# The recurrence's products in another shape, merge parts between its stages, and modulation pieces moved later, in a one-layer attention, recurrence and feed-forward block

## The chip, the cores and the metric

One Trainium2 chip, one NeuronCore. The metric is the device time of one execution of the program, in microseconds (us). TensorE (PE in the profile) multiplies; VectorE (DVE) and ScalarE (ACT) do the elementwise work; SyncE (SP) only issues the transfers; GpSimd (POOL) has nothing to do.

## The reference, cut to what matters

All numbers are float32, for 256 tokens of width 2048. The conditioning vector `c` gives six modulation rows of 2048 numbers, and the token mixer has two branches, an attention (three kinds of it, added with gates) and a gated linear recurrence, whose outputs are merged:

```python
c_act = jax.nn.silu(c)
mod = c_act @ ada_w[l] + ada_b[l]                  # 2048 x 12288
sh1, sc1, g1, sh2, sc2, g2 = jnp.split(mod, 6)
h = rmsnorm(x, norm1_g[l]) * (1.0 + sc1) + sh1
# token mixer
z = h @ w_in                                       # 2048 x 13360
q, kc, vc, ks, vs, kw, vw, g_nsa, lx, ly, ga, gb = jnp.split(z, ...)
o_a = nsa_attention(q, kc, vc, ks, vs, kw, vw, g_nsa, ...)
u = causal_dwconv(lx, conv_w, conv_b)
o_b = jax.nn.gelu(ly) * rg_lru(u, w_a, b_a, w_i, b_i, lam)
merged = jax.nn.sigmoid(ga) * (o_a @ proj_a) + jax.nn.sigmoid(gb) * (o_b @ proj_b)
y = merged @ w_out
# and behind it
x = x + g1 * y
h = rmsnorm(x, norm2_g[l]) * (1.0 + sc2) + sh2
x = x + g2 * conv_glu_ffn(h, ffn_up[l], ffn_conv_w[l], ffn_conv_b[l], ffn_down[l])
return rmsnorm(x, final_g)
```

`rg_lru` makes two gates from `u` by 128-wide blocks, and from them the coefficients of a scan over the tokens.

## The kernel before, in words

**Numbers.** A float32 product is made of three products in a shorter format that the array takes in one pass: each operand is a high part `hi` (ACT's copy into the short format) and a low part `lo` (DVE's difference), and hi·hi, hi·lo and lo·hi are added in PSUM. An activation such as `h1` holds its two parts side by side, columns 0 to 255 and 256 to 511.

**Weights.** Every weight comes once, in pieces of 128 x 2048 numbers (1 MB): `stage` takes one of four `raw` slots and `load` issues the transfer on SyncE's queue, in program order. `split` makes `hi` and `lo` of half a piece (L107 ACT, L108 DVE), in three buffers each, at a raised priority. `bank` gives one of four PSUM banks of 512 columns.

**Products.** `dense_pair` (feed-forward, L114) makes for each 128 x 128 block of weights one product of `hi` with all 512 columns and one of `lo` with 256; the two 256-column halves of a bank are added later (`reduce`). Its order is fixed by `keep_in_program_order`. `dense_pair1` (L172, used 16 times, by the recurrence alone) makes three products of 256 columns for each block, two of `hi` and one of `lo`, into one bank for both of its outputs f. `dense_tok` (L192) has the tokens as the stationary operand and 512 columns of weights moving, 96 products for a call with four pieces.

**Modulation.** `ada_piece` (L232) stages one piece of `ada_w` in a `raw` slot, and DVE multiplies it with the row of `silu(c)` and sums (L234), then adds the offset (L235). `filler(n)` takes the next n of 64 pieces of the list `fill`, in the order g1, sc2, sh2, g2. The rows have due times: g1 and sc2 before the output projection ends its first part, sh2 before the feed-forward part, g2 behind it.

**Order.** A planner orders each engine's instructions ahead of time by priority, which is program order, and by when operands and slots are free; a queue is worked off in that order. Behind the first projections come four query products with an attention unit each, then eight rounds `pr` of a recurrence input `lx` (`dense_pair1`), a further attention unit in the first four, and `filler(2)`. `attention(g, t)` makes scores for four heads, one after the other, softmax (L676 to L686), transposes, and the product with the values into `oA`. Then four recurrence stages `bt` run: convolutions on DVE (L740, L743), gate products (L745, L747), Sigmoid, Tanh, Exp and Sqrt on ACT in an order fixed by `tbl` (each kind needs its table loaded), the scan (L762), and two rounds of `ly` with Gelu into `oB`. The merge loops over four column blocks n and the branches s: gates (for n = 0 they were made earlier and lie in `mq`), Sigmoid (L792), the product with `oA` or `oB`, `filler`, and behind both the sum and its transposes. The output projection (four `dense_tok`) adds to x, squares, and writes the transposed result into `hp`.

**Slots.** SBUF tiles of one tag share one place. C0 to C7 hold in turn the compressed keys' operands (`gat`, `gath`), `cmpb`, the probabilities' transposes `pT`, the recurrence's `lx` (C4 to C7) and `oB`.

## Time and profile before

| | |
|---|---|
| median of 3 runs | 1792.68 us (1792.08 to 1794.26) |
| the profiled execution | 1793.77 us |
| its span | 1792.0 us |
| instructions | 25746 |
| mean TensorE clock granted | 0.997 of 2.4 GHz |
| read from HBM | 425.72 MB, 239 GB/s over the span |

The span is the time from the first to the last instruction of the program in the profiled execution; the rest of its time lies around it. In the profile a line such as L107 or L53 can be that of a helper (`split`, `load`), and the names are those of the tiles. Products overlap in the array and their ends are modelled, so the distance from start to start tells more than a duration. PEld is the load of the stationary operand, which runs beside the products.

### The profile page before, as it was taken

To read this page: it belongs to the slowest core of one execution; us is meant where nothing else is said; L and a number is where in the kernel's file an instruction comes from. 1 tells how busy PE (TensorE), PEld (TensorE's weight loads), DVE (VectorE), ACT (ScalarE), POOL (GpSimd) and SP (SyncE) were. 2 spreads that over 40 slices of the span, in tenths; PEclk is the share of its full clock that TensorE was granted. 3 is DMA by queue.
4 is the path that set the end of the run, shared out by engine and by line. 5 is a ranking of instruction groups with operands and counts; after the bars stand their busy time and mean duration, and the time that the engine had idled before them with its cause. 6 is when DMAs were issued, how large, how long until landed. Compare 5 with 4: busy or idle time off the path is not lost.

```text
span 1792.0 us, 25746 instructions
## 1 busy us (share of the span) xinstructions
PE 1771.6 (99%) x10262; PEld 1545.9 (86%) x10262; DVE 1350.5 (75%) x1976; ACT 881.9 (49%) x1202; POOL 0.2 (0%) x4
## 2 busy tenths in 40 slices
PE   8999999999999999999999999999999999999997
PEld 7999898888999888888888998888888888888886
DVE  7998897998698766767765997888555677766555
ACT  5644464655578444444445644444433444444443
POOL 0000000000000000000000000000000000000000
PEclk9999999999999999999999999999999999999999
DMA  9999864665646867777775566777655555555552
GB/s 350 379 335 355 288 245 161 235 212 203 221 173 227 303 237 290 286 292 281 294 266 195 186 235 235 282 282 282 239 193 200 191 188 188 188 188 188 190 198 106
DMA packets 64200, 429.50 MB, mean 240 GB/s; under 512 B 7088, under 2 KB 7376, under 8 KB 15568
## 3 DMA queue, kind: packets, MB, share of 16 engines
q1 hardware_dynamic: 63792, 427.08, 66.2%
q8 instruction: 80, 1.31, 0.3%
q10 hardware_dynamic: 288, 0.79, 0.1%
q14 instruction: 40, 0.33, 0.1%
HBM read 425.72 MB, written 2.11 MB: 239 GB/s over the span
## 4 chain that ended last, share of the span: by engine, by line
PE 86%; DVE 6%; DMA 4%; issue 2%; ACT 2%; SPq 0%; DVEq 0%; ACTq 0%
PE P L130 26%; PE P L204 12%; PE P L205 12%; PE P L203 12%; PE P L187 3%; PE P L188 3%; PE P L185 3%; DMA raw<-ada_w 2%; DVE lo L108 2%; PE P L464 2%; PE P L466 2%; PE P L465 2%; PE P L149 1%; PE P L148 1%; PE P L150 1%
## 5 line engine op out<-in xcount | busy, mean ns | idle before, releaser
L107 ACT ACTIVATE hi<-raw 128x1024 fp32r<-128x1024 f32 x588 | 622.0, 1060 | 764.5 <-PE P L205 325.5
L108 DVE TENSOR_TENSOR lo<-raw,hi 128x1024 fp32r<-128x1024 f32 x588 | 717.1, 1222 | 370.5 <-ACT hi L107 369.7
L130 PE MATMUL P<-h,hi 128*128 128x512 f32 x1344 | 463.9, 394 | 0.0
L130 PE MATMUL P<-h,lo 128*128 128x256 f32 x1344 | 366.4, 278 | 0.0
L130 PEld LDWEIGHTS P<-h,hi 128*128 128x128 f32 x1344 | 249.1, 188 | 54.9
L130 PEld LDWEIGHTS P<-h,lo 128*128 128x128 f32 x1344 | 252.4, 188 | 4.2
L234 DVE SCALAR_TENSOR_TENSOR raw<-raw,crow 128x2048 f32<-128x2048 f32 x64 | 146.2, 2285 | 3.6 <-DMA raw<-ada_w 3.2
L188 PE MATMUL P<-h,lo 128*128 128x256 f32 x512 | 147.6, 289 | 0.8 <-DVE lo L108 0.8
L187 PE MATMUL P<-h,hi 128*128 128x256 f32 x512 | 146.7, 287 | 0.0
L185 PE MATMUL P<-h,hi 128*128 128x256 f32 x512 | 146.7, 287 | 0.0
L464 PE MATMUL P<-h,hi 128*128 128x256 f32 x384 | 107.9, 285 | 0.3 <-ACT hi L107 0.3
L465 PE MATMUL P<-h,hi 128*128 128x256 f32 x384 | 107.6, 284 | 0.0
L466 PE MATMUL P<-h,lo 128*128 128x256 f32 x384 | 102.2, 284 | 0.0
L188 PEld LDWEIGHTS P<-h,lo 128*128 128x128 f32 x512 | 97.8, 191 | 1.8 <-DVE lo L108 1.4
L187 PEld LDWEIGHTS P<-h,hi 128*128 128x128 f32 x512 | 97.9, 191 | 1.4 <-issue 1.2
L185 PEld LDWEIGHTS P<-h,hi 128*128 128x128 f32 x512 | 97.9, 191 | 1.0 <-issue 0.7
L204 PE MATMUL P<-lo,ua 128*128 128x512 f32 x240 | 93.5, 390 | 0.3 <-DVE lo L108 0.3
L205 PE MATMUL P<-hi,ua 128*128 128x512 f32 x240 | 93.4, 389 | 0.0
L203 PE MATMUL P<-hi,ua 128*128 128x512 f32 x240 | 83.6, 389 | 0.0
L204 PE MATMUL P<-lo,h 128*128 128x512 f32 x192 | 75.5, 393 | 0.0
L464 PEld LDWEIGHTS P<-h,hi 128*128 128x128 f32 x384 | 74.0, 193 | 1.1 <-ACT hi L107 0.5
L205 PE MATMUL P<-hi,h 128*128 128x512 f32 x192 | 74.9, 390 | 0.0
(281 smaller groups left out, 3131.6 us busy)
## 6 DMA issues: line engine op xcount, KB each, us to landing
raw<-ada_w SPq DMA_DIRECT2D x96, 1024.0 KB, 5.0
raw<-w_up SPq DMA_DIRECT2D x96, 1024.0 KB, 4.8
raw<-w_down SPq DMA_DIRECT2D x48, 1024.0 KB, 4.9
raw<-w_lru SPq DMA_DIRECT2D x32, 1024.0 KB, 4.9
raw<-w_proj SPq DMA_DIRECT2D x32, 1024.0 KB, 5.1
raw<-w_gates SPq DMA_DIRECT2D x24, 1024.0 KB, 6.5
raw<-w_out SPq DMA_DIRECT2D x16, 1024.0 KB, 4.9
raw<-w_kv SPq DMA_DIRECT2D x24, 512.0 KB, 6.7
```

Of the source, the lines that this page charges most:

```text
L107: A.activation(hi[:, :n], raw[:, lo_col:lo_col + n], AF.Copy)
L108: V.tensor_tensor(lo[:, :n], raw[:, lo_col:lo_col + n], hi[:, :n].bitcast(F32), op=ALU.subtract)
L130: PE.matmul(ps[f][:, 0:256] if w else ps[f], hl[w][:, k * 256 + f * 128:k * 256 + f * 128 + 128], r[:, 0:256] if w else r, start=(kt == 0 ...
L185: PE.matmul(o, hi[:, sl], r[:, 0:256], start=(kt == 0 and f == 0), stop=False, skip_group_check=True)
L187: PE.matmul(o, hi[:, sl], r[:, 256:512], start=False, stop=False, skip_group_check=True)
L188: PE.matmul(o, lo[:, sl], r[:, 0:256], start=False, stop=(kt == n - 1), skip_group_check=True)
L203: PE.matmul(ps[j], xh, hi[:, w], start=(kt == 0), stop=False, skip_group_check=True)
L204: PE.matmul(ps[j], xh, lo[:, w], start=False, stop=False, skip_group_check=True)
L205: PE.matmul(ps[j], xl, hi[:, w], start=False, stop=(kt == n - 1), skip_group_check=True)
L234: V.scalar_tensor_tensor(raw, raw, 1.0, row, op0=ALU.mult, op1=ALU.mult, accum_out=modc[:, c:c + 1])
L464: PE.matmul(o, hi[:, sl], h1[:, kt, 0:256], start=first and f % 2 == 0, stop=False, skip_group_check=True)
L465: PE.matmul(o, hi[:, sl], h1[:, kt, 256:512], start=False, stop=False, skip_group_check=True)
```

## The change

It touches six things. `dense_pair1` goes; the recurrence's 16 products are made by `dense_pair` with `pinned=False`, which leaves their order to the planner, and `add_halves` takes each bank out with a copy on ACT and an addition on DVE. The first merge parts move up between the recurrence stages: behind the scan of stages 0 and 2 the product of branch 0 with `oA` for n = 0 and 1, behind that of stages 1 and 3 the gates for n = 1; their Sigmoids, and those of `mq`, are put into the `tbl` order behind the next stage's Tanh. The modulation pieces are called for inside `dense_tok`, behind the weight pieces that `fills` lists, and fewer of them early: 24 are left behind the merge instead of 16. In attention, the heads' probabilities are scaled and transposed in pairs, with max, reciprocal and gate once for each pair. `cmpb` goes to C3, `gat` to C7, `gath` to C2, C4, C5 and C6; `w2t`, `hs`, the first head's `p` and `gp` share one buffer `xp` of twice the size instead of two. The last columns of `hp` are written behind the output projection instead of ahead of it.

```diff
-        def dense_pair(pieces, rhs):
+        def dense_pair(pieces, rhs, pinned=True):
...
-                    for w in (0, 0, 1, 0, 1, 0, 1, 1) + (0, 1) * 4 if ip + half == 0 else (0, 1) * 8:
+                    for w in (0, 0, 1, 0, 1, 0, 1, 1) + (0, 1) * 4 if pinned and ip + half == 0 else (0, 1) * 8:
...
+                        if pinned:
+                            tc.keep_in_program_order(mm)
             return ps
+
+        def add_halves(dst, p):
+            A.activation(dst, p[:, 256:512], AF.Copy)
+            with tc.high_priority(200):
+                V.tensor_tensor(dst, p[:, 0:256], dst, op=ALU.add)
...
-        def dense_pair1(pieces, rhs):
...
-        def dense_tok(pieces, lhs, late=None):
+        def dense_tok(pieces, lhs, late=None, fills=()):
...
                     for j in range(2):
                         products(j, k0, *hl)
+                if ip in fills:
+                    filler()
...
-        cmpb = big.tile([128, 1024], F32R, tag="C7", name="cmpb")
+        cmpb = big.tile([128, 1024], F32R, tag="C3", name="cmpb")
...
-        w2t = tmp.tile([128, 2, 128], F32, tag="xp", bufs=2, name="w2t")
+        wh = tmp.tile([128, 2, 256], F32, tag="xp", bufs=1, name="wh")
+        w2t = wh[:, 0].rearrange("p (j e) -> p j e", j=2)
...
-                g = big.tile([128, 16, 4, NCMP], F32, tag="C6", name="gat")
+                g = big.tile([128, 16, 4, NCMP], F32, tag="C7", name="gat")
...
+            def turn_heads(hh):
+                p = heads[hh]
+                for b in range(2):
+                    pb = p[:, b * nk:b * nk + nk]
+                    V.tensor_scalar(pb, pb, sm[:, 1, hh, b:b + 1], None, op0=ALU.mult)
+                tp = psx.tile([128, 512], F32, tag="t", bufs=1, name="tp")
+                for j in range(nj):
+                    PE.transpose(tp[:, j * 128:j * 128 + 128], p[:, j * 128:j * 128 + 128], ident)
+                for n in range(t + 1):
+                    A.activation(pT[n][:, :, hh, :], tp[:, n * 256:n * 256 + 256].rearrange("p (j q) -> p j q", q=128),
+                                 AF.Copy)
...
+                p = tmp.tile([128, 512], F32, tag=("xp", "r", "iu", "tt")[hh], bufs=1, name="p")
...
+                if hh % 2 == 0:
+                    continue
+                w = sm[:, 1, hh - 1:hh + 1]
+                V.tensor_scalar(w, w, 1e-30, None, op0=ALU.max)
+                V.reciprocal(w, w)
+                V.tensor_tensor(w, w, gates[:, hh - 1:hh + 1, 1:3], op=ALU.mult)
+                turn_heads(hh - 1)
+                turn_heads(hh)
...
         for pr in range(8):
-            pl = dense_pair1([w_lru[pr, k] for k in range(2)], h1r)
...
+            ps = dense_pair([w_lru[pr, k] for k in range(2)], h1r, False)
+            for f in range(2):
+                add_halves(lx[pr // 2][:, 2 * (pr % 2) + f], ps[f])
             if units:
                 attention(*units.pop(0))
-            filler(2)
+            filler()
...
+        def gates_of(n, s, fills):
+            if n == 0:
+                gated[n, s] = [mq[s][:, j] for j in range(2)]
+                return gated[n, s]
+            gated[n, s] = [tmp.tile([128, 512], F32, tag=(("r", "iu"), ("u", "tt"))[s][j], bufs=1, name="sg")
+                           for j in range(2)]
+            return dense_tok([w_gates[n - 1, s, k] for k in range(4)], h1r, fills=fills)
+
+        def open_gates(n, s, ps):
+            for j in range(2):
+                tbl(A.activation(gated[n, s][j], ps[j], AF.Sigmoid))
+
+        def multiply(n, s, fills):
+            rhs = (lambda kt: oB[kt // 2][:, kt % 2]) if s else (lambda kt: oA[:, kt])
+            ps = dense_tok([w_proj[n, s, k] for k in range(4)], rhs, fills=fills)
+            for j in range(2):
+                V.tensor_tensor(gated[n, s][j], ps[j], gated[n, s][j], op=ALU.mult)
+
+        waiting = [(0, s, gates_of(0, s, ())) for s in range(2)]
...
+            while waiting:
+                open_gates(*waiting.pop(0))
             tbl(A.activation(r, r, AF.Exp, scale=-2.0))
...
+            if bt % 2 == 0:
+                multiply(bt // 2, 0, (1,))
+            else:
+                waiting.append((1, bt // 2, gates_of(1, bt // 2, (1,))))
             for h in range(2):
...
-                pl = dense_pair1([w_lru[8 + pr, k] for k in range(2)], h1r)
+                ps = dense_pair([w_lru[8 + pr, k] for k in range(2)], h1r, False)
                 gl = u[:, 2 * h:2 * h + 2]
-                tbl(A.activation(gl, pl.rearrange("p (f t) -> p f t", f=2), AF.Gelu_apprx_tanh))
+                for f in range(2):
+                    add_halves(gl[:, f], ps[f])
+                tbl(A.activation(gl, gl, AF.Gelu_apprx_tanh))
...
-                filler(2 if pr % 4 == 0 else 0)
...
+            for s in range(2):
+                if (n, s) not in gated:
+                    open_gates(n, s, gates_of(n, s, (1, 3) if s else (0, 1, 3)))
+                if s == 1 or n > 1:
+                    multiply(n, s, (0, 1, 3))
...
-        filler(max(0, len(fill) - 16))
+        assert len(fill) == 24
...
-            ps = dense_tok([w_out[n, k] for k in range(4)], lambda kt: mg[kt // 2][:, kt % 2])
+            ps = dense_tok([w_out[n, k] for k in range(4)], lambda kt: mg[kt // 2][:, kt % 2],
+                           fills=(0, 1, 3) if n < 2 else (0, 2) if n == 2 else ())
...
-                    gp = tmp.tile([128, 256], F32, tag="xp", bufs=2, name="gp")
+                    gps = tmp.tile([128, 2, 256], F32, tag="xp", bufs=1, name="gp") if f == 0 else gps
+                    gp = gps[:, f]
```

## Rows read from the trace of the kernel before

**Rows 1.** The page of the profile: busy time, share of the span and instructions of each engine; and from the 40 slices the TensorE clock granted, in tenths of full speed (2.4 GHz).
```profile
PE 1771.6 (99%) x10262; PEld 1545.9 (86%) x10262; DVE 1350.5 (75%) x1976; ACT 881.9 (49%) x1202; POOL 0.2 (0%) x4
...
PEclk9999999999999999999999999999999999999999
```

**Rows 2.** The page: the chain of work that ended last, share of the span by engine.
```profile
PE 86%; DVE 6%; DMA 4%; issue 2%; ACT 2%; SPq 0%; DVEq 0%; ACTq 0%
```

**Rows 3.** The view of waits, TensorE alone, whole span: line and tile that waited, for what; us in total, times, the longest one.
```profile
PE P L255 <- DVE dg L253: 4.8, 1, 4.8
...
PE P L188 <- DVE lo L108: 0.8, 2, 0.7
PE tp L689 <- ACT pcT L661: 0.5, 1, 0.5
```

**Rows 4.** Busy time by stretches. The columns are: from:to and length in us; busy us and instructions of TensorE products (PE), of its weight loads (PEld), of DVE, ACT and POOL; TensorE clock granted; share of the DMA engines; GB/s.
```profile
20.00:200.00 180.00, 176.85 (x1309) 169.13 (x1310) 163.59 (x172) 96.22 (x136) 0.00 (x0) 0.99 0.94 350
285.00:475.00 190.00, 189.50 (x1306) 160.59 (x1305) 165.26 (x446) 109.94 (x267) 0.00 (x0) 1.00 0.56 200
475.00:590.00 115.00, 114.18 (x884) 111.25 (x884) 96.74 (x136) 88.30 (x116) 0.00 (x0) 1.00 0.61 215
590.00:900.00 310.00, 310.00 (x1380) 256.04 (x1379) 217.92 (x244) 131.62 (x146) 0.00 (x0) 1.00 0.78 285
900.00:990.00 90.00, 90.00 (x437) 75.43 (x436) 55.55 (x70) 46.70 (x69) 0.00 (x0) 1.00 0.62 222
1050.00:1250.00 200.00, 200.00 (x1164) 175.29 (x1163) 175.65 (x254) 88.99 (x102) 0.00 (x0) 1.00 0.74 267
```

**Rows 5.** The order of time, TensorE, in a stretch where only the recurrence's products run: start in us, duration, line, what is written and read. Between the two rows lie 26 more products of 256 columns.
```profile
447.30 0.28 PE L185 MATMUL P<-h,hi 128*128 128x256 f32 x1
...
450.54 0.28 PE L185 MATMUL P<-h,hi 128*128 128x256 f32 x1
```

**Rows 6.** The chain that ended last, in order of time, merged: start, length, line, count. First a stretch of the feed-forward part; then two places of the merge, five half pieces apart (12 products each).
```profile
1385.19 266.87 PE P L130 x1536
...
700.65 0.45 PE P L203 x2
714.25 0.45 PE P L203 x2
```

**Rows 7.** Groups of instructions by line, kept apart by shape: line, engine, operation, what is written and read, shapes, count | busy us, mean ns of one | idle time of the engine before them and what ended it.
```profile
L832 DVE TENSOR_TENSOR res<-res,yg 128x512 f32<-128x512 f32 x24 | 15.5, 682 | 0.1
...
L892 ACT ACTIVATE fgl<-ct 128x512 f32<-128x512 f32 x24 | 15.1, 628 | 5.1 <-DVE ct L889 5.0
...
L852 DVE SCALAR_TENSOR_TENSOR hp<-turn,modc,hp 128x256 fp32r<-128x256 f32 x16 | 7.1, 478 | 1.0 <-ACT hp L851 1.0
...
L809 DVE TENSOR_TENSOR mg<-turn,mg 128x256 fp32r<-128x256 f32 x16 | 6.0, 415 | 0.0
...
L808 ACT ACTIVATE mg<-turn 128x256 fp32r<-128x256 f32 x16 | 5.2, 377 | 2.8 <-PE turn L806 2.8
L681 DVE TENSOR_SCALAR sm<-sm 128x2 f32<-128x2 f32 x32 | 5.2, 162 | 3.3 <-ACT p L679 3.2
...
L716 ACT ACTIVATE lx<-P 128x512 f32<-128x512 f32 x8 | 4.6, 579 | 0.0
```

**Rows 8.** The order of time, DVE, with a modulation piece (L234, L235) and a split (L108).
```profile
331.08 2.28 DVE L234 SCALAR_TENSOR_TENSOR raw<-raw,crow 128x2048 f32<-128x2048 f32 x1
...
333.82 0.15 DVE L235 TENSOR_TENSOR modc<-modc,cols 128x1 f32<-128x1 f32 x1
333.89 1.22 DVE L108 TENSOR_TENSOR lo<-raw,hi 128x1024 fp32r<-128x1024 f32 x1
335.03 0.20 DVE L649 TENSOR_REDUCE st<-pc 128x4 f32<-128x60 f32 x1
```

**Rows 9.** The order of time, TensorE, at its three latest starts between 300 and 590 us: the product before each gap and the one behind it.
```profile
328.36 0.28 PE L188 MATMUL P<-h,lo 128*128 128x256 f32 x1
329.14 0.66 PE L689 MATMUL tp<-cols,p 128*128 128x128 f32 x4 [0.50 <-ACT pcT L661]
...
516.47 0.28 PE L187 MATMUL P<-h,hi 128*128 128x256 f32 x1
516.91 0.39 PE L188 MATMUL P<-h,lo 128*128 128x256 f32 x1 [0.17 <-DVE lo L108]
...
551.78 0.28 PE L187 MATMUL P<-h,hi 128*128 128x256 f32 x1
552.71 0.38 PE L188 MATMUL P<-h,lo 128*128 128x256 f32 x1 [0.65 <-DVE lo L108]
```

**Rows 10.** The order of time, ACT, around the first of these.
```profile
326.20 1.28 ACT L792 ACT_TABLE_LOAD   x1
...
328.50 0.58 ACT L661 ACTIVATE pcT<-tpc 47x512 fp32r<-47x512 f32 x1
```

**Rows 11.** The order of time, ACT: the last copy of an attention output and the last copy of a recurrence input.
```profile
474.79 0.60 ACT L701 ACTIVATE oA<-oT 128x512 fp32r<-128x512 f32 x1 [3.58 <-PE oT L697]
...
480.30 0.58 ACT L716 ACTIVATE lx<-P 128x512 f32<-128x512 f32 x1
```

**Rows 12.** The DMA view from 20 to 200 us: GB/s in 40 slices, and the modulation pieces issued there (count, KB each, median us to landing).
```profile
GB/s 309 408 415 333 360 370 327 353 389 407 336 420 406 390 377 291 360 304 346 231 355 357 359 369 367 332 352 410 377 338 309 395 328 377 335 315 335 222 317 309
...
raw<-ada_w SPq DMA_DIRECT2D x27, 1024.0 KB, 7.0
```

More of the change, by code (lines that the diff above doesn't have):

```diff
@@ L170, in up @@
             return take
-        def dense_pair1(pieces, rhs):
-            p = bank()
-            n = len(pieces) * 8
-            for ip, ap in enumerate(pieces):
-                raw = stage(ap)
-                for half in range(2):
-                    hi, lo = split(raw, half * 1024, 1024)
-                    for f in range(2):
-                        o = p[:, f * 256:f * 256 + 256]
-                        for k in range(4):
-                            kt = ip * 8 + half * 4 + k
-                            sl = slice(k * 256 + f * 128, k * 256 + f * 128 + 128)
-                            r = rhs(kt)
-                            PE.matmul(o, hi[:, sl], r[:, 0:256], start=(kt == 0 and f == 0), stop=False,
-                                      skip_group_check=True)
-                            PE.matmul(o, hi[:, sl], r[:, 256:512], start=False, stop=False, skip_group_check=True)
-                            PE.matmul(o, lo[:, sl], r[:, 0:256], start=False, stop=(kt == n - 1),
-                                      skip_group_check=True)
-            return p
-        def dense_tok(pieces, lhs, late=None):
+        def dense_tok(pieces, lhs, late=None, fills=()):
             ps = [bank(), bank()]
@@ L413, in compress @@
                 return
-            hs = tmp.tile([128, 4, 64], F32, tag="xp", bufs=2, name="hs")
+            hs = wh[:, 1].rearrange("p (g n) -> p g n", g=4)
             V.memset(hs, 0.0)
@@ L664, in attention @@
             nj = 2 * (t + 1)
+            sm = tmp.tile([128, 2, 4, 2], F32, tag="sm", bufs=2, name="sm")
+            heads = []
+            def turn_heads(hh):
[9 more added lines that the diff above has]
+                                 AF.Copy)
             for hh in range(4):
@@ L677, in attention @@
-                V.tensor_scalar(sm[:, 0:2], sm[:, 0:2], -SCALE, None, op0=ALU.mult)
-                for b in range(2):
-                    A.activation(p[:, b * nk:b * nk + nk], s[:, b * nk:b * nk + nk], AF.Exp, bias=sm[:, b:b + 1],
-                                 scale=SCALE, accum_out=sm[:, 2 + b:3 + b])
-                V.tensor_scalar(sm[:, 2:4], sm[:, 2:4], 1e-30, None, op0=ALU.max)
-                V.reciprocal(sm[:, 2:4], sm[:, 2:4])
-                V.tensor_tensor(sm[:, 4:6], sm[:, 2:4], gates[:, hh, 1:3], op=ALU.mult)
@@ new lines, in attention @@
+                V.tensor_reduce(sm[:, 0, hh], s[:, 0:2 * nk].rearrange("p (b n) -> p b n", b=2), axis=AX, op=ALU.max)
+                V.tensor_scalar(sm[:, 0, hh], sm[:, 0, hh], -SCALE, None, op0=ALU.mult)
+                for b in range(2):
+                    A.activation(p[:, b * nk:b * nk + nk], s[:, b * nk:b * nk + nk], AF.Exp, bias=sm[:, 0, hh, b:b + 1],
+                                 scale=SCALE, accum_out=sm[:, 1, hh, b:b + 1])
+                heads.append(p)
+                if hh % 2 == 0:
+                    continue
@@ L772, in block_kernel @@
                 V.tensor_tensor(oB[pr][:, :, 256:512], gl, oh.bitcast(F32), op=ALU.subtract)
-                filler(2 if pr % 4 == 0 else 0)
+        while waiting:
+            open_gates(*waiting.pop(0))
         row1 = None
@@ L855, in block_kernel @@
                 tc.keep_in_program_order(A.activation(warm, col("eps"), AF.Sqrt))
+        for n in range(8):
+            sh = modc[:, 48 + 2 * n:50 + 2 * n].unsqueeze(2).to_broadcast([128, 2, 2])
+            A.activation(hp[n][:, :, 0, 256:258], sh, AF.Copy)
+            V.tensor_tensor(hp[n][:, :, 1, 256:258], sh, hp[n][:, :, 0, 256:258].bitcast(F32), op=ALU.subtract)
         rstd(sdev, sums)
-        dr = tmp.tile([128, 2, 128], F32, tag="xp", bufs=2, name="dr")
+        dr = tmp.tile([128, 2, 128], F32, tag="xp", bufs=1, name="dr")
         for j in range(2):
```

48 lines of the change are left out of this document (6 added, 42 removed).

## Prediction

> **What bounds the kernel now.** I read the share of busy time and the slices first [rows 1]: TensorE is busy 1771.6 of 1792.0 us, at its upper clock level of 2.4 GHz in every slice; VectorE (DVE) comes second with 75%. A busy share says little where ends of products are modelled, so the chain of work that ended last comes next [rows 2]: 86% of it is TensorE, 6% DVE. Then TensorE's own list of waits [rows 3]: 4.8 us and the other large items lie in the first stages, and behind 285 us, where the change begins to act, the view names 0.8 us for a late lo half and 0.5 us for a late pcT. By stretches [rows 4], TensorE is busy in 189.5 of 190 us from 285 to 475 (attention with the recurrence's input products between), in 114.2 of 115 us up to 590 (the recurrence), and without a break from 590 to 990 (merge, then output projection). So each product that is shortened there is time won, and what another engine gains is worth nothing unless TensorE waited for it. DVE in the same stretches: 165.3 of 190, 96.7 of 115, 217.9 of 310, 55.6 of 90. It is close to its limit early and has room later.
>
> **The recurrence's products.** dense_pair1 issues three 256-wide products for each 128x128 block; dense_pair issues one 512 wide and one 256 wide for the same sums. Durations overlap, so I take start to start. In an undisturbed run of the old form, 27 steps go from 447.30 to 450.54, 3.24 us, 120.0 ns each, 360 ns for a block [rows 5]. The new form runs already in the feed-forward part: 1536 products in 266.87 us, half of them of each width, 173.7 ns each, 347.5 ns for a block [rows 6]. Difference 12.5 ns. Blocks: 16 calls x 2 pieces x 2 halves x 8 = 512. Removed 184.3 us, added 177.9 us: **-6.4 us**, all of it on the engine that sets the end.
>
> The page "TensorE: Matmul & The Clock Gate" of the Trainium skill, section "Back-to-back issue gap", gives N/2.4 + 2.5 ns from one product to the next. By it a block is 327.5 ns the old way and 325.0 ns the new way, and the sum would be -1.3 us instead of -6.4: what it has for a product fewer is the 2.5 ns alone. The rows disagree with it, 360 and 347.5 ns. What it would do here is a rival below.
>
> **The evacuation** grows: instead of one ACT copy of 512 columns for a call (579 ns) there are two ACT copies of 256 and two DVE additions, nearest 377 and 415 ns [rows 7]; eight calls get a Gelu of their own, nearest 628 ns. DVE +32 x 0.415 = 13.3 us, ACT +32 x 0.38 + 8 x 0.63 - 16 x 0.58 = +7.9 us, spread over 16 calls. What hides it: TensorE works on the other bank. A call holds two of the four banks instead of one. Where gates_of(1, s) holds the other two until its Sigmoid, the next call needs the bank just finished, but a call works 4 blocks on the first bank (1.4 us) before it touches the second, about what a copy and an addition take. Without that cover it is up to 1 us for each of the four calls concerned; I take 0, bound 0 to +4.
>
> **Modulation pieces.** 64 in all, before and after. In the first stretch 8 instead of 16, in the recurrence 4, in the merge 28, in the output projection 8, then 16 as before. A piece costs DVE 2.21 + 0.07 us, start to start, a lo half 1.14 us [rows 8]. So DVE is spared 8 x 2.28 = 18 us up to 475 us. It is also spared 1 us in each attention unit: max, reciprocal and gate, 0.16 us each [rows 7], run for two heads at once, two sets fewer a unit, 8 x 2 x 0.48 = 7.7 us. Against 13.3 us added over both stretches this is relief, worth nothing directly, since TensorE is busy throughout.
>
> **The stalls it can remove.** Three places. At 328.36 a product is followed at 329.14 by the next, 0.78 us instead of 0.12, because the pcT copy was late [rows 9]; ahead of it ACT did a table load and a Sigmoid for the merge's mq tile [rows 10], which the change ties behind Tanh in the first recurrence stage, where that table is loaded anyway: -0.66 us. At 551.78 and at 516.47 the next product follows after 0.93 and 0.44 us, because a lo half is late [rows 9]: 0.81 and 0.32 us over the 0.12, together 1.1 us; DVE was between convolutions and splits there. In the new order each recurrence stage has a merge product of 21.8 us between (8 halves of 2.72 us [rows 6]), more TensorE time for the same DVE work. I take half, -0.55, bounds 0 and -1.1. Next late after these would be the recurrence's own gate products, which nothing waits for at once.
>
> **The added waits.** On ACT, the Sigmoid of gates (1, 0) stands in stage 2 between Tanh and Exp, that of (1, 1) behind the last Gelu. Behind them in ACT's queue are Exp, Sqrt and the hi halves that TensorE needs. The product that each waits for was called a stage, or two ly calls (2 x 32 x 0.35 = 22 us), earlier, which hides it: 0; if it came late, TensorE has up to three hi and lo halves in hand, 2.7 us each, so the bound is some +2. The number of table loads falls by the early one above and the load back to Exp, 1.28 us each [rows 10], off the path but for that one stall. On TensorE, multiply(0, 0) waits for all of oA: a rival below.
>
> **At nothing.** The slots (cmpb and gat change names; p of head 0 and hs go to xp, whose two 1 KB buffers become one of 2 KB): lx[3] no longer waits for the end of attention, and nothing new shares a slot while in use; in the feed-forward part gp's only writers and readers are DVE, in order. The eight small columns of hp go behind the projection: 16 short ACT and DVE instructions before the first feed-forward product, whose splits are in by then; bound +1.5 us.
>
> **Merge and projection, fuller.** DVE in one projection product with three pieces: 8 x 1.14 + 3 x 2.28 + 4 x 0.68 + 4 x 0.48 = 20.6 us [rows 7, 8] of 21.8 and the transposes: 92%, bound on DVE if slips add up. The feed-forward stretch ran at 175.7 of 200 us without a stall [rows 4]. Transfers: from multiply(0, 1) to the third projection product 2 x 7 + 2 x 27 + 2 x 7 = 82 pieces of 1.049 MB in 12 x 21.8 = 262 us, 328 GB/s. The stretch 20 to 200 us moved 350 GB/s [rows 4], so I take 0; the merge so far showed only 285.
>
> **Sum** against the profiled execution's 1793.77 us (span 1792.0): -6.4 - 0.66 - 0.55 = -7.6, 1786.2 us. The median of the runs is 1792.68, 1.1 lower, so I forecast **1785.0 us**; its own range is 1781 to 1789.
>
> **Rivals.**
> *Attention outlasts the products between it* (0.14). The last oA copy starts at 474.79, the last lx copy at 480.30 [rows 11]: today the fillers last 5.5 us longer than attention. They shrink by 8 x 32 x 12.5 ns = 3.2 us, and heads turned in pairs put one more head's transposes and copies (0.4 + 2 x 0.38 us, [rows 7] for the copy's like) at the end of each unit, some 9 us over eight. What is staged next is multiply(0, 0), which needs all of oA, and the loads behind it stand in SyncE's one queue, so ly's products can't step in as they could before. If DVE's relief of 18 us does not shorten attention, TensorE waits 9 + 3.2 - 5.5 = 7 us less attention's own work, some 4: 1789. For it: one more stage of order; against: DVE was at 87% in that stretch, and its delays are what attention's short chain waits for.
>
> *A block keeps nearly its old length* (0.06). The array's own part, 768 columns at 2.4 GHz, is 320 ns in both forms; what is over, 40 and 28 ns [rows 5, 6], I count by the product. If it were paid otherwise, by the change from one accumulating bank to the other or by the turn to attention's products and back, a block here would shorten by 0 to 3 ns, at most 1.5 us in all, and with the stalls the time is about 1790.5. The Trainium skill's rule named above gives -1.3 us, which is this case. Against it: [rows 6] is the same engine on operands of the same kinds.
>
> *The fuller stages run short of data* (0.12, the other side). A late modulation piece stands in DVE's order ahead of a lo half, and its slot, one of four, holds back the next weight piece on SyncE's queue. For it: landing takes 7.0 us at 350 GB/s [rows 12] where the four slots have to turn in 4 x 21.8 / 7 = 12.4 us. It decides below 321 GB/s, where 86.0 MB take 268 us and 6 us of the gain are gone; at 310 GB/s it is 277 us, +15, 1800; at the merge's present 285 it would be +40, the far bound, though there TensorE and not the transfers set the pace. Against: [rows 12] shows many slices above 350.
>
> *All gaps close* (0.07): stalls too short for the view of waits go as well, below 1782.
>
> **Chances.** My forecast 0.58, the four rivals 0.39, the rest 0.03. About 0.2% (3.6 us) is what a measurement can tell from no change. Faster by more: 0.58 + 0.07 + 0.04 of the first rival = 0.69. Within: 0.10 of the first, the second's 0.06, a quarter of the third, some of the rest: 0.21. Slower: 0.10. Range 1781 to 1794: it leaves out the slow case's larger part and most of the last one.
>
> **What would show it.** Blocks of lx and ly at 347 to 349 ns start to start; TensorE's instructions fewer by 512; no Sigmoid load near 320 and 326 us; no wait of TensorE over 0.5 us between 285 and 600; a DMA share of 0.85 to 0.92 and still no wait on lo from then to the end of the projection; the feed-forward part of the same length. The prediction is wrong if TensorE idles before the first product on oA, or if in the merge products begin on DVE lo or a DMA.

## The result: slower by 1%, and the profile after

The changed kernel takes 1812.4 us (1807.4 to 1814.5), the kernel before 1792.7 us: ratio 1.0105, interval 1.0083 to 1.0126. The forecast was 1785.0 us, with a range from 1781 to 1794. The profiled execution has a span of 1810.9 us, 18.9 more than before.

The page of the profile after: engines, chain by engine and by line, and the group of the modulation pieces (L223; idle time of DVE just before them at the end of the line).
```profile
PE 1777.1 (98%) x9750; PEld 1519.5 (84%) x9750; DVE 1358.5 (75%) x1960; ACT 885.9 (49%) x1224; POOL 0.2 (0%) x4
...
PE 75%; DMA 11%; DVE 9%; issue 3%; ACT 1%; DVEq 0%; SPq 0%; ACTq 0%
PE P L129 35%; DMA raw<-ada_w 10%; PE P L191 7%; PE P L192 7%; PE P L190 7%; DVE lo L108 3%; DVE raw L223 2%; PE P L456 2%; PE P L454 2%; PE P L455 2%; PE P L155 1%; PE P L154 1%; PE P L156 1%; PE s L672 1%; PE oT L695 1%
...
L223 DVE SCALAR_TENSOR_TENSOR raw<-raw,crow 128x2048 f32<-128x2048 f32 x64 | 146.5, 2289 | 53.0 <-DMA raw<-ada_w 52.8
```
TensorE has its 512 instructions fewer, yet its share of the chain fell from 86% [rows 2] to 75%; DMA took its place, and in it the modulation pieces' transfers, for which DVE now waits 53 us, in 34 waits (3.2 us before).

The loss lies ahead of the feed-forward part. Its first products, before (L148) and after (L154), duration ns min/median/max, first and last start in us:
```profile
L148 PE MATMUL P<-hp,hi x192: 278/282/363, 984.0 to 1053.8; 128*128 128x258 f32 x192
```
```profile
L154 PE MATMUL P<-hp,hi x192: 278/282/363, 1003.5 to 1073.3; 128*128 128x258 f32 x192
```
They start 19.5 us later; from there to the end it is 808.0 us before and 807.4 after. By stretches (columns as in [rows 4]), after:
```profile
285.00:475.00 190.00, 190.00 (x1085) 151.12 (x1085) 150.19 (x383) 105.69 (x262) 0.00 (x0) 1.00 0.47 169
475.00:600.00 125.00, 117.64 (x562) 96.00 (x561) 89.55 (x133) 82.37 (x115) 0.00 (x0) 0.97 0.51 185
600.00:700.00 100.00, 96.33 (x471) 80.15 (x470) 67.43 (x79) 55.93 (x69) 0.00 (x0) 0.98 0.57 207
700.00:930.00 230.00, 226.69 (x1003) 184.38 (x1002) 176.25 (x205) 94.60 (x110) 0.00 (x0) 1.00 0.84 317
```
From 285 to 475 us TensorE has no break. Then TensorE idles 11 us in the recurrence, at a lower mean clock, and 3 us in the merge, where it had no break before [rows 4]. Its waits from 475 to 700 us, then from 700 to 1000 us:
```profile
PE P L191 <- DVE lo L108: 7.1, 4, 3.2
PE P L129 <- DVE lt L139: 2.0, 1, 2.0
PE P L190 <- ACT hi L107: 1.8, 2, 1.2
```
```profile
PE P L191 <- DVE lo L108: 3.3, 7, 1.1
```

Three kinds of wait are in these lines. The longest stands in multiply(1, 0), between the second and the third stage. TensorE, ACT and DVE there, in order of time (rows of each left out between):
```profile
588.93 0.73 PE L190 MATMUL P<-hi,oA 128*128 128x512 f32 x2 [1.19 <-ACT hi L107]
592.91 0.80 PE L191 MATMUL P<-lo,oA 128*128 128x512 f32 x1 [3.25 <-DVE lo L108]
```
```profile
579.23 1.06 ACT L107 ACTIVATE hi<-raw 128x1024 fp32r<-128x1024 f32 x1 [0.68 <-DVE lt L139]
...
582.56 1.28 ACT L771 ACT_TABLE_LOAD   x1
...
587.41 0.51 ACT L772 ACTIVATE lt<-lru_i,cols 128x256 f32<-128x256 f32 x1
587.77 2.99 ACT L107 ACTIVATE hi<-raw 128x1024 fp32r<-128x1024 f32 x3
```
```profile
589.33 1.21 DVE L780 TENSOR_TENSOR lt<-lt 128x1024 f32<-128x1024 f32 x1
590.46 1.26 DVE L763 SCALAR_TENSOR_TENSOR lt<-lx,cols,lt 128x253 f32<-128x253 f32 x3
591.64 1.22 DVE L108 TENSOR_TENSOR lo<-raw,hi 128x1024 fp32r<-128x1024 f32 x1
```
The stage's burst (table load, eight Sigmoids and a Tanh behind the last Gelu) stands on ACT ahead of three hi halves: from the start of one half (579.23) to that of the next (587.77) 8.5 us pass, and a half lasts TensorE 2.7 us [rows 6]. Then the lo half waits 2.8 us more on DVE, behind the stage's product and convolutions. The second kind is a bank (line `DVE lt L139`): at 669.7 us the addition of ly's halves stands behind a modulation piece of 2.29 us, while gates_of(1, 1) holds two banks (its Sigmoid starts at 689.6). The third is in the merge; DVE, then TensorE:
```profile
856.40 2.29 DVE L223 SCALAR_TENSOR_TENSOR raw<-raw,crow 128x2048 f32<-128x2048 f32 x1 [3.79 <-DMA raw<-ada_w]
...
858.62 1.22 DVE L108 TENSOR_TENSOR lo<-raw,hi 128x1024 fp32r<-128x1024 f32 x1
```
```profile
859.89 0.50 PE L191 MATMUL P<-lo,oA 128*128 128x512 f32 x1 [1.08 <-DVE lo L108]
```
DVE waits for a piece's transfer, and the lo half behind it in the fixed order waits with it.

These waits are not the whole loss. The idle time from 475 to 930 us is 14.3 us, 0.8 before. By the granted clock of the stretches above, the slower clock makes some 5 us more, and the shorter products give 3.8 us back (worked out below). That is some 15 of the 19.5 us; the other 4 or so stand in no line read here.

### The profile page after: what moved, and what is told of

It reads as the page before. It is cut to its first block, busy times and chain, and to the rows that moved or that the text cites. A ratio compares the mean times of both kernels' runs of the same rounds, so it can differ in the third digit from the quotient of the medians.

```text
span 1810.9 us, 24673 instructions
## 1 busy us (share of the span) xinstructions
PE 1777.1 (98%) x9750; PEld 1519.5 (84%) x9750; DVE 1358.5 (75%) x1960; ACT 885.9 (49%) x1224; POOL 0.2 (0%) x4
## 4 chain that ended last, share of the span: by engine, by line
PE 75%; DMA 11%; DVE 9%; issue 3%; ACT 1%; DVEq 0%; SPq 0%; ACTq 0%
PE P L129 35%; DMA raw<-ada_w 10%; PE P L191 7%; PE P L192 7%; PE P L190 7%; DVE lo L108 3%; DVE raw L223 2%; PE P L456 2%; PE P L454 2%; PE P L455 2%; PE P L155 1%; PE P L154 1%; PE P L156 1%; PE s L672 1%; PE oT L695 1%
## 5 line engine op out<-in xcount | busy, mean ns | idle before, releaser
L108 DVE TENSOR_TENSOR lo<-raw,hi 128x1024 fp32r<-128x1024 f32 x588 | 714.7, 1221 | 311.6 <-ACT hi L107 310.9
L129 PE MATMUL P<-h,hi 128*128 128x512 f32 x1856 | 647.4, 396 | 2.0 <-DVE lt L139 2.0
L129 PE MATMUL P<-h,lo 128*128 128x256 f32 x1856 | 510.0, 280 | 0.0
L129 PEld LDWEIGHTS P<-h,hi 128*128 128x128 f32 x1856 | 345.0, 188 | 77.0 <-DVE lt L139 2.3
L129 PEld LDWEIGHTS P<-h,lo 128*128 128x128 f32 x1856 | 349.8, 188 | 7.3 <-issue 1.0
L223 DVE SCALAR_TENSOR_TENSOR raw<-raw,crow 128x2048 f32<-128x2048 f32 x64 | 146.5, 2289 | 53.0 <-DMA raw<-ada_w 52.8
L454 PE MATMUL P<-h,hi 128*128 128x256 f32 x384 | 108.2, 286 | 0.8 <-ACT hi L107 0.8
L455 PE MATMUL P<-h,hi 128*128 128x256 f32 x384 | 107.8, 285 | 0.0
L454 PEld LDWEIGHTS P<-h,hi 128*128 128x128 f32 x384 | 73.8, 192 | 1.5 <-ACT hi L107 1.2
L192 PE MATMUL P<-hi,h 128*128 128x512 f32 x192 | 74.9, 390 | 0.0
L455 PEld LDWEIGHTS P<-h,hi 128*128 128x128 f32 x384 | 73.9, 192 | 0.0
L312 DVE SCALAR_TENSOR_TENSOR raw<-raw,crow 128x2048 f32<-128x2048 f32 x31 | 70.6, 2283 | 3.0 <-DMA raw<-ada_w 2.9
L456 PEld LDWEIGHTS P<-h,lo 128*128 128x128 f32 x384 | 70.4, 191 | 0.3 <-issue 0.2
L190 PE MATMUL P<-hi,h 128*128 128x512 f32 x192 | 68.0, 391 | 0.6 <-ACT hi L107 0.6
L191 PE MATMUL P<-lo,oA 128*128 128x512 f32 x128 | 52.0, 406 | 4.8 <-DVE lo L108 4.8
L155 PE MATMUL P<-hp,hi 128*128 128x258 f32 x192 | 54.0, 284 | 0.0
```

The source lines that it names most:

```text
L108: V.tensor_tensor(lo[:, :n], raw[:, lo_col:lo_col + n], hi[:, :n].bitcast(F32), op=ALU.subtract)
L129: mm = PE.matmul(ps[f][:, 0:256] if w else ps[f], hl[w][:, k * 256 + f * 128:k * 256 + f * 128 + 128], r[:, 0:256] if w else r, start=(kt ...
L155: PE.matmul(o, hi[:, sl], r[:, 1], start=False, stop=False, skip_group_check=True)
L190: PE.matmul(ps[j], xh, hi[:, w], start=(kt == 0), stop=False, skip_group_check=True)
L191: PE.matmul(ps[j], xh, lo[:, w], start=False, stop=False, skip_group_check=True)
L192: PE.matmul(ps[j], xl, hi[:, w], start=False, stop=(kt == n - 1), skip_group_check=True)
```

## Experiments

All ratios are to the kernel before on the same chip. "Parts" are the four merge products between the stages, "pieces" the modulation pieces.

**Width alone, and each of the two moves undone.** Theory A: parts cost. Theory B: pieces inside products cost.

`e1_width`, kernel before with
```
-            pl = dense_pair1(...)          # all 16 calls, lx and ly
+            ps = dense_pair(..., h1r, False)
+            for f in range(2): add_halves(..., ps[f])
```


> The kernel before with one part of the change alone: the recurrence's 16 products in the 512 and 256 wide form with their halves added by ACT and DVE; no merge part moved, modulation pieces, slots and attention as before. If the width gains what the trace of after shows (512 blocks shorter by about 10.5 to 12.5 ns) and its evacuation is hidden, 1786 to 1788 us, some 5 to 6 under the kernel before. If the wider form's two banks a call or the added DVE and ACT work are part of the loss, 1790 us or more.

Measured: 1802.2 us, 1.0046 (1.0031 to 1.0061). Neither: the width alone is slower.

`e2_behind`, changed kernel with
```
-            if bt % 2 == 0: multiply(bt // 2, 0, (1,))
-            else: waiting.append((1, bt // 2, gates_of(1, bt // 2, (1,))))
...
+                multiply(n, s, (0, 1, 3) if s or n > 1 else (1,))
```


> The changed kernel with the four merge parts put back behind the recurrence, each with its own modulation piece inside; all else as changed. Theory A: a merge part between two recurrence stages makes TensorE wait, since the stage's burst of Sigmoid, Tanh, Exp, Sqrt and convolutions stands ahead of its hi and lo halves. Then the 12.5 us of waits and most of the 4.5 us of slower clock between 540 and 690 us go: about 1797 to 1799 us. Theory B: what costs is the modulation pieces inside the products, wherever these stand. Then little changes: 1808 to 1812 us.

Measured: 1815.6 us, 1.0122 (1.0107 to 1.0137).

`e3_bursts`, changed kernel with
```
-                if ip in fills: filler()      # no fills anywhere
+            filler(2)                         # behind each lx call
+                filler(2 if pr % 4 == 0 else 0)
+                filler(2 if n == 0 else 4)
```


> The changed kernel with the modulation pieces back in the places of before: two behind each input product of the recurrence, two in stages 1 and 3, bursts of two and four behind the merge products, none inside a product; the merge parts stay between the stages. Theory A (merge parts between stages make the waits): only the merge's and projection's 5.5 us and perhaps a slot come back, 1803 to 1808 us. Theory B (the pieces inside the products make them): about 1790 to 1795 us.

Measured: 1815.1 us, 1.0113 (1.0096 to 1.0130).

`e4_both`: both edits.

> The changed kernel with both undone: merge parts behind the recurrence and modulation pieces in the places of before; left of the change are the width, the slots, attention's heads in pairs, the early Sigmoid of the merge's first gates and the later columns of hp. If A and B together are the whole loss, it is as the kernel before with the width alone, 1785 to 1788 us. If slots or pairs cost something, it stands above that kernel by as much. If A and B add, its gain over the changed kernel is the sum of the gains of the two kernels that undo one each; if they are one cause (a slot held by a piece in a merge part), it is less.

Measured: 1805.7 us, 1.0067 (1.0052 to 1.0082). Undoing one of the two moves gains nothing, undoing both gains 7 us, and what is left is 3.5 us slower than the width alone: slots, pairs, early Sigmoid and late hp columns, the rest of the change, are not free. The larger part, 8 us, is there with the width alone, so there is a third cause. In this kernel one wait stands out, from 490 to 600 us:
```profile
PE P L129 <- DVE lt L139: 7.4, 1, 7.4
```

**Theory C: ly's evacuation.** The 7.4 us are a wait for a bank: ACT's copies of the halves stand behind a whole burst and write the stage's tile u. Four kernels go at this.

`e5_ly_old` (changed kernel) and `e6_both_ly_old` (e4_both): ly as before,
```
+                pl = dense_pair1([w_lru[8 + pr, k] for k in range(2)], h1r)
+                tbl(A.activation(gl, pl.rearrange("p (f t) -> p f t", f=2), AF.Gelu_apprx_tanh))
```


> The changed kernel with the recurrence's output-side products (ly) back in the form of three 256 wide products in one bank, one Gelu from the bank; its input-side products (lx) stay wide, merge parts and modulation pieces as changed. Theory C: the wide form of ly is the main cost, because a call holds two of four banks, and its halves are copied by ACT into the stage's own tile u behind the stage's burst. Then the waits at 542, 589, 649 and 670 us (12.5 us with 4.5 us of slower clock) go for the most part, and 2.7 us of the width are given back: 1797 to 1801 us. Theory A (a merge part between the stages is late by itself): only the wait of 2.2 us for a bank goes, 1811 to 1815 us.

> The kernel with merge parts and modulation pieces as before the change (1805.7 us), ly's products moreover in the old form; lx stays wide, slots and attention's pairs as changed. Theory C: the 16 us lost between 500 and 600 us, 7.4 of them one wait for a bank, are gone, less 2.7 us of the width: 1788 to 1792 us, a little under the kernel before. If lx, the slots or the pairs make the loss, it stays at 1800 us or more.

`e7_both_own_tile` (e4_both) and `e8_own_tile` (changed kernel): the halves added by one DVE reduction,
```
+                gl = tmp.tile([128, 2, 256], F32, tag=..., bufs=1, name="gl")
+                for f in range(2): reduce(gl[:, f], ps[f])
```


> The same kernel of 1805.7 us with ly wide, but its halves are added by one DVE reduction straight from the bank, as the feed-forward part does it, into a tile of its own instead of the stage's tile u; no ACT copy. Theory C: the bank comes free as soon as the products end, no wait over 0.5 us between 500 and 600 us, and the whole width is won: 1785 to 1788 us. If two banks a call are too few whatever the evacuation, 1795 us or more.

> The changed kernel with the same evacuation of ly (one DVE reduction into a tile of its own), all else as changed. Theory C: 1794 to 1799 us, the merge's and projection's 5.5 us being left. Theory A: the wait for a bank at 670 us goes, those at 542, 587 to 593 and 649 us stay: 1807 to 1811 us.

Measured: 1805.4 (1.0058), 1808.3 (1.0076), 1807.0 (1.0075) and 1809.6 us (1.0081), each within 0.0017. With the two moves undone, C falls: in e6_both_ly_old no bank is waited for, but from 475 to 700 us TensorE waits for halves instead:
```profile
PE P L191 <- ACT hi L107: 9.0, 5, 4.2
PE P L194 <- DVE lo L108: 3.6, 3, 1.8
```
There the bank wait was a symptom. In the changed kernel C holds in part. e5_ly_old lies between the two forecasts, 8.4 us under the changed kernel (1.0058 against 1.0105, intervals apart), and is the only kernel with a single edit that gains clearly; e8_own_tile gains 4 us, within the intervals. In e5_ly_old TensorE waits 5.1 us from 475 to 700 us, where the changed kernel waits 10.9 and e6_both_ly_old 12.6:
```profile
PE P L211 <- DVE lo L108: 4.2, 3, 2.4
PE P L210 <- ACT hi L107: 0.9, 1, 0.9
```
So with ly old and lx wide the two moves together cost nothing (1805.4 us with them, 1808.3 without, same chip). What is left in all four kernels is 10 us and more; they share lx in the wide form.

**Theory D: lx's width moves the order.** The copies of attention's outputs, in the kernel before and in e1_width (duration ns, first and last start), each with the lx blocks issued between: one product of L185 a block before, two of L129 a block after.
```profile
L701 ACT ACTIVATE oA<-oT x8: 580/598/603, 328.0 to 474.8; 128x512 fp32r<-128x512 f32 x8
```
```profile
328.00:474.80 146.80, 68.84 (x240) 45.60 (x239) 1.00 0.58 205
```
```profile
L687 ACT ACTIVATE oA<-oT x8: 578/592/601, 326.2 to 491.6; 128x512 fp32r<-128x512 f32 x8
```
```profile
326.20:491.60 165.40, 109.73 (x548) 85.02 (x546) 0.97 0.56 205
```
The planned order puts 274 blocks (548 / 2) beside seven units where it put 240. lx has 256, so at least 18 are ly's, spent beside attention, which ends 17 us later (in e4_both 24 us: last copy at 499.2). The recurrence's tiles (D0 to D5) are those of attention's queries, keys and values, so by theory D it starts late, with less product time to cover it.

`f1_ly_wide`: kernel before, ly alone wide.

> The kernel before with ly alone in the wide form and its added halves; lx as before. Theory D: the loss comes from lx. With lx wide, the planned order puts some 46 blocks of products between two attention units where it put 33, so attention ends at 492 to 500 us instead of 475, ly's products are spent ahead of it, and the recurrence, which starts when attention has given its tiles back, has too little left to cover its stages. With lx as before attention ends at 475 us, TensorE waits for nothing over 1 us up to 600 us, and ly's 256 blocks give 2.7 us: 1789 to 1792 us. Theory C (ly's two banks and its evacuation cost by themselves): 1797 us or more.

Measured: 1793.3 us, 0.9996 (0.9986 to 1.0005); attention ends at 473.9 us. With lx old the loss is gone. lx alone wide, with nothing else changed, was not run; e6_both_ly_old has it wide beside ly old, with slots, pairs and the rest as changed, and loses 13.6 us. ly's 256 blocks gain nothing either: TensorE's waits from 300 to 600 us have 1.9 us of late lo halves, against 0.8 before [rows 3]:
```profile
PE P L129 <- DVE lo L108: 1.9, 2, 1.4
```

`f2_width_paced` (e1_width), `f3_both_paced` (e4_both), `f4_after_paced` (changed kernel):
```
+            with tc.issue_after(ends[pr].ins):     # last product of attention unit pr
                 ps = dense_pair([w_lru[pr, k] for k in range(2)], h1r, False)
```


> The kernel with the width alone (1802.2 us), and each lx call's products told to stand, in TensorE's order, behind the last product of the attention unit of the same number, so that an attention unit has 32 blocks beside it as before the change had 33. Nothing else is altered. Theory D: attention ends near 475 us again, the waits from 465 to 600 us go, and the width's gain shows: 1786 to 1789 us. If the pace of attention isn't the cause, or TensorE now waits for attention's own chain: 1795 us or more.

> The kernel of 1805.7 us (merge parts and modulation pieces as before; wide products, slots, attention's pairs) with the same order of lx and attention. Theory D: 1784 to 1789 us; attention's last copy near 475 us; no wait over 1 us from 480 to 600 us. Otherwise 1795 us or more.

> The changed kernel with the same order of lx and attention; merge parts between the stages and pieces inside products as changed. Theory D: attention ends near 475 us and the waits at 542 to 593 us shrink; the 5.5 us of late lo halves in merge and projection stay: 1793 to 1802 us. If merge parts between the stages are late by themselves, the waits of 12 us stay and it is 1808 us or more.

Measured: 1801.1 (1.0041, 1.0026 to 1.0056), 1805.2 (1.0054, 1.0037 to 1.0071) and 1821.1 us (1.0148, 1.0132 to 1.0165). In f2_width_paced attention ends at 476.2 us, and TensorE's idle time from 490 to 600 us falls from 3.4 us (e1_width) to 2.1; in f3_both_paced, where attention ends at 478.5, from 13.3 (e4_both) to 6.1. So the recurrence waits less, as D says, but from 285 to 490 us the idle time rises from 4.1 to 6.5 and from 0 to 7.0, inside attention. TensorE's waits in f2_width_paced from 300 to 490 us, then from 490 to 600:
```profile
PE oT L683 <- ACT pT L677: 3.1, 3, 1.4
PE sc L626 <- ACT p L665: 2.3, 2, 1.4
PE s L653 <- DVE pc L630: 1.1, 3, 0.4
```
```profile
PE P L129 <- DVE lo L108: 1.4, 2, 1.0
```
So the runs bear out D's link from attention's end to the recurrence's waits, but this order only moves the waits, and the times that D forecast do not come. In f4_after_paced attention ends at 474.1 us and the kernel is slower still: in the changed kernel an early end of attention cures nothing. There A and B had to be tried without D.

**The moves with lx in the old form.** Four kernels, all with ly wide, slots, pairs, early Sigmoid and late hp columns as changed:
```
+            pl = dense_pair1([w_lru[pr, k] for k in range(2)], h1r)
+            A.activation(lx[...], pl.rearrange("p (f t) -> p f t", f=2), AF.Copy)
```
`g1_lx_old`: parts and pieces as changed.

> The changed kernel with lx back in the old form (three 256 wide products in one bank, one ACT copy); ly wide, merge parts between the stages and pieces inside products as changed. Theory D (late attention is the cause): attention ends near 475 us, and the time is 1793 to 1800 us. Theory A (merge parts between the stages make TensorE wait by themselves, and pieces inside products cost 5.5 us in merge and projection): the waits of some 12 us between 540 and 690 us stay, 1806 to 1813 us.

`g2_bursts_lx_old`: pieces as before.

> The same kernel (lx old, merge parts between the stages) with the modulation pieces in the places of before. Theory A: the between-stage waits stay, 1803 to 1811 us. If it is the pieces inside products that make them (a slot held, a DVE wait in front of a lo half), 1792 to 1796 us. Theory D: 1792 to 1796 us too.

`g3_both_lx_old`: parts and pieces as before.

> The same kernel with both undone: lx old, ly wide, merge parts and pieces as before; of the change are left ly's width, the slots, attention's heads in pairs, the early Sigmoid and the late hp columns. Where none of these costs, it is as the kernel before with ly wide alone: 1791 to 1795 us. Over 1797 us one of them costs.

`g4_behind_lx_old`: parts as before, pieces inside products.

> The changed kernel with lx in the old form and the merge parts behind the recurrence; pieces stay inside products. Against the same kernel with the pieces in the old places (1796.5 us) it shows what the pieces inside products cost by themselves. If they cost the 5 to 9 us of late lo halves that the merge and projection of the changed kernel show: 1802 to 1806 us. If they cost only together with parts between the stages, 1795 to 1799 us.

Measured: 1819.9 (1.0145, 1.0127 to 1.0162), 1818.6 (1.0139, 1.0124 to 1.0154), 1796.5 (1.0014, 1.0005 to 1.0024) and 1803.1 us (1.0051, 1.0034 to 1.0068). With the first kernels this makes a table of the excess over the kernel before (ratio less one, times 1793 us), each good to 3 or 4 us; ly is wide in every row:

| | pieces as before | pieces inside |
|---|---|---|
| lx old, parts behind the recurrence | 2.5 | 9.1 |
| lx old, parts between the stages | 24.9 | 26.0 |
| lx wide, parts behind | 12.0 | 21.9 |
| lx wide, parts between | 20.3 | 18.8 (the change) |

With lx old and ly wide, parts between the stages cost 17 to 22 us: there theory A holds. With lx wide they cost 8 us where the pieces are as before, and nothing where the pieces are inside. With ly old beside it (theory C above) parts and pieces together cost nothing. No kernel has the parts between the stages with both lx and ly old, so whether a part costs by itself, or only beside ly's two banks and added halves, is open. Pieces inside products cost 7 to 10 us where the parts are behind, and nothing to be seen where the parts are between. lx's width costs 10 to 13 us where the parts are behind and gives 5 to 7 back where they are between. The terms do not add. TensorE's waits from 475 to 700 us without the moves (g3_both_lx_old), then with both (g1_lx_old):
```profile
PE P L129 <- DVE lo L108: 2.9, 3, 1.3
PE P L129 <- DVE lt L139: 1.9, 1, 1.9
```
```profile
PE P L211 <- DVE lo L108: 7.1, 6, 3.2
PE P L210 <- ACT hi L107: 5.1, 3, 3.3
PE P L129 <- DVE lt L139: 2.0, 1, 2.0
```
The wait of 3.25 us on lo in multiply(1, 0) is there to the hundredth in g2_bursts_lx_old too, which has no piece inside that product:
```profile
594.70 0.80 PE L211 MATMUL P<-lo,oA 128*128 128x512 f32 x1 [3.25 <-DVE lo L108]
```
So this wait comes from neither the piece nor the slot that it holds. That g2_bursts_lx_old is no faster has a reason of its own: from 475 to 760 us it also waits 5.7 us, once, for the sum of the two branches of n = 0 on DVE (L842; the transposes, L847, wait for it). That sum and the multiplication ahead of it stand behind modulation pieces of the burst, three of them from 702.6 to 711.3 us. e3_bursts has the same wait, 5.8 us.

`h1_lx_wide_paced`: kernel before, lx alone wide, with
```
+            ps = dense_pair([w_lru[pr, k] for k in range(2)], h1r, False, [marks[pr][2 + 2 * j] for j in range(2)])
             # piece j behind marks[pr][2 + 2 * j]: third head's scores; the unit's last product
```


> The kernel before with lx alone in the wide form (ly old), and a looser order: the first piece of each lx call behind the third head's scores of the attention unit of the same number, the second behind that unit's last product; this plans 34 to 47 blocks to a unit and the end of attention at block 248 of 256, before the change it was 243. Theory D: attention ends near 478 us, TensorE waits little in it, and lx's 2.7 us of width and the 0.66 us wait for pcT show: 1789 to 1792 us. If the order again makes TensorE wait for attention's chain, 1795 to 1800 us.

Measured: 1796.3 us, 1.0014 (1.0005 to 1.0024). Attention ends at 478.7 us. That is 2.5 us over the kernel before, where e1_width lost 8.2 and f2_width_paced 7.4; ly alone wide equals the kernel before, so most of lx's loss lay in the planned order and comes back with another. Attention's chain still shows (1.4 us for p, 1.4 for late hi halves up to 600 us), and the width's gain does not appear.

**Is it the order of burst and halves?** `k1_part_ahead`, changed kernel:
```
         for bt in range(4):
+            while waiting: open_gates(*waiting.pop(0))
+            if bt % 2 == 0: multiply(bt // 2, 0, (1,))
+            else: waiting.append((1, bt // 2, gates_of(1, bt // 2, (1,))))
...
-            while waiting: open_gates(*waiting.pop(0))
...
-            if bt % 2 == 0: multiply(bt // 2, 0, (1,))
-            else: waiting.append((1, bt // 2, gates_of(1, bt // 2, (1,))))
```


> The changed kernel with each merge part written ahead of its stage instead of behind it, with the Sigmoid of the gates that it needs; the work and the places of the pieces are the same, but the planner now puts hi halves between a stage's Sigmoids (2 to 4 of them where there were none or all eight Sigmoids in a row). If the order of burst and halves makes the waits, those of 3.0, 4.8 and 1.6 us at 542, 587 to 593 and 649 us shrink to under 1.5 us each and the time falls to 1797 to 1804 us. If the parts' transfers, slots or banks make them, they stay, 1809 to 1815 us.

Measured: 1815.7 us, 1.0119 (1.0104 to 1.0134). The longest wait for hi is gone, as expected, but the sum from 475 to 700 us is the same (12 us, after 10.9):
```profile
PE P L191 <- DVE lo L108: 4.0, 2, 2.3
PE P L129 <- DVE lo L108: 3.8, 5, 1.0
PE P L129 <- DVE lt L139: 3.5, 1, 3.5
PE P L129 <- ACT hi L107: 0.6, 1, 0.6
```
One reading is that the burst delays either the part's halves or ly's; it is not shown. Open stays which shortage sets the sum, the three buffers of hi and lo or the order on DVE; no kernel with more buffers was tried. No version was faster than the kernel before; ly wide alone equals it.

## Why the prediction was wrong, step by step

Three steps failed: a width's gain taken to reach the end, the parts taken as cover, and ly's evacuation put at 0. Their costs are shown by kernels that leave each out, but do not add; the shortage behind them is open.

- *The recurrence's products, -6.4 us.* The kind of gain was right, its size too high. In the chain of after 128 products in a row, 64 blocks, take 352.5 ns a block, not 347.5:
```profile
608.74 22.56 PE P L129 x128
```
  That is 7.5 of 12.5 ns, 3.8 us in 512 blocks. The prediction's estimate from N/2.4 + 2.5 ns, which the Trainium skill's page "TensorE: Matmul & The Clock Gate", section "Back-to-back issue gap", gives for an isolated product, was 2.5 ns a block; the trace shows three times that. What failed is "all of it on the engine that sets the end": with parts behind, lx's width changed the planned order and cost 10 to 13 us, and e1_width ended 8 us slower.
- *The stalls it can remove.* The pcT wait of 0.66 us did go. The parts as cover are the second step: "In the new order each recurrence stage has a merge product of 21.8 us between ..., more TensorE time for the same DVE work. I take half, -0.55". It counted sums of work, but the merge product brought its own halves into the queue behind the burst. In place of -0.55 stand 17 to 22 us with lx old and ly wide. With ly old and lx wide, waits from 475 to 700 us did fall with the two moves, from 12.6 to 5.1 us, so the idea is not wrong in every kernel.
- *Merge and projection, fuller, 0.* With parts behind, the pieces inside cost 7 to 10 us. The slow rival named the right mechanism, a late piece ahead of a lo half, but tied it to bandwidth below 321 GB/s. From 700 to 930 us the changed kernel ran at 317 GB/s, where by the prediction's sum 86.0 MB would take 9 us longer than the products; TensorE lost 3.3 us in waits for lo, behind pieces in DVE's fixed order. The rest of the 7 to 10 us is not taken apart.
- *The evacuation, 0, bounds 0 to +4.* The third step that failed. In the changed kernel the one wait for a bank is 2.0 us, but e5_ly_old, with ly in one bank and no halves to add, is 8.4 us faster although its products are some 1.9 us longer: outside the bounds. With the halves added another way (e8_own_tile) 4 us come back, within the intervals. In e4_both one wait for a bank is 7.4 us.
- *Attention outlasts the products.* In after attention's last copy starts at 500.4 us instead of 474.8, but TensorE did not wait for it up to 475 us or at the first product on oA: other products filled in. multiply(0, 0) starts at 468.4 us, ahead of that copy: it takes oA part by part, where the rival had it need all of oA. Nor does an early end help: g1_lx_old, with the last copy at 469.1 us, is slower than the changed kernel.
- *At nothing.* Slots, pairs, early Sigmoid and hp columns together cost some 3 us: g3_both_lx_old stands 3.2 us above f1_ly_wide, e4_both 3.5 above e1_width. Not taken apart.
- *What would show it.* 512 instructions fewer, the feed-forward part of the same length: right. "No wait of TensorE over 0.5 us between 285 and 600" and "still no wait on lo from then to the end of the projection": wrong. Products of the merge that begin on DVE lo were the sign named for a wrong prediction, and they came.

## What to carry to other kernels

Work moved between two stages brings its own operand halves into the same in-order queues; before counting it as cover, list what stands ahead of each half on ACT and DVE, and how long TensorE's stock of halves lasts. Where a planner writes the order, a shorter product changes the order of everything that was interleaved with it, so try each width alone, before and apart from any move. When undoing the large moves one by one gains nothing, undo them in pairs, and undo the small edits too: causes can hide one another, and here the one single edit that gained was ly's old form.

## What the runs showed of the hardware

TensorE's clock fell to its lower level after some waits and not after others. Stretches of after (columns as above): behind a wait of 2.83 us at 545.2 us; from the two waits of 1.19 and 3.25 us on; behind 2.01 us at 672.0 us.
```profile
545.10:550.00 4.90, 4.79 (x21) 3.97 (x22) 4.68 (x9) 4.83 (x5) 0.00 (x0) 1.00 0.59 214
...
589.00:594.00 5.00, 1.75 (x5) 1.12 (x6) 5.00 (x9) 4.98 (x7) 0.00 (x0) 0.73 0.12 16
594.00:598.00 4.00, 4.00 (x11) 3.13 (x10) 4.00 (x7) 3.37 (x4) 0.00 (x0) 0.50 0.85 328
...
672.00:676.00 4.00, 4.00 (x15) 3.47 (x16) 2.68 (x5) 1.79 (x3) 0.00 (x0) 0.65 1.01 418
```
The granted clock stayed at 1.00 behind 2.83 us and fell behind 2.01; 0.73 and 0.65 are means over stretches at both levels. By these figures the 4 us at 0.50 (1.2 GHz) cost another 2 us, the 4 us at 0.65 another 1.4, some 3.4 us with the wait of 2.01 us ahead of them.
